# The first row maximum inside the gated unit's stage, gate inputs in token tiles, and base tiles loaded by SP's queue

## The chip, the cores and the metric

The kernel runs on one core of a Trainium2 chip. The time is device microseconds of one execution of the whole program on that core; the figure for a kernel is the median over several executions. The engines are PE (matrix multiplications), DVE (VectorE), ACT (ScalarE), POOL (GpSimd) and SP, which here only issues transfers. SP, ACT and POOL each issue DMAs, in the order of the program.

## The reference

One encoder layer over 2048 tokens of width 1024, with 16 learned meta tokens ahead of them, in float32:

```python
h = layer_norm(concat([meta, x]))
proj = h @ w_in
q, k, v, u, g_attn, g_ssm = split(proj)
q, k = apply_rope(rms_norm(q)), apply_rope(rms_norm(k))
y_attn = block_attention(q, k, v)             # 8 heads, 2 heads of keys and values, softmax over 2064 tokens
y_ssm = s5_branch(u, ...)                     # diagonal state space, then y * sigmoid(y @ w_glu + b)
merged = sigmoid(g_attn) * (y_attn @ w_attn_br) + sigmoid(g_ssm) * (y_ssm @ w_ssm_br)
h = layer_norm(ALPHA * h + merged @ w_o)
moe = sum over 16 experts of the top 256 tokens of each: (silu(t @ w_gate) * (t @ w_up)) @ w_down
out = layer_norm(ALPHA * h + moe)[16:]
```

## The kernel before

Each float32 operand of a large product is split into a high part (copied by ACT) and a low part (what DVE or POOL subtracts), and three matmuls (high by high, high by low, low by high) make one product. So ahead of each block of matmuls stand a cast on ACT and a subtraction on DVE, and ahead of these a DMA of the weights. The stages follow each other in one program; within an engine, instructions run in the order in which the code emits them, and generators (`yield`) interleave the stages by hand.

`phase_a` (0 to 300 us) norms the token tiles of 128 tokens (`ln_ops`, two `scalar_tensor_tensor` lines L106 and L107 at its end), transposes them (`trans`), and multiplies them by the columns for q, k, v (`qkv`, column group 0) and for u (`u_mm`, column group 1). `split_w(p, k)` splits the weights of column group p and row block k (L157). After the first pair of tiles a loop over `s` runs as a pipeline: transpose tile s+1, `qkv(s)`, norm of s+2, rotary positions of s-1 (`rope`), stores of s-3.

`gates` is the product for the two gates: 64 blocks of 24 matmuls of 512 columns (`pg`, L1230). It yields after every four matmuls, and the other stages call for such a quantum (`next(gg)`) wherever PE would otherwise stand, up to the first scores of attention. Its inputs are loaded back from `ht_d` in 256 KB pieces by SP.

`ssm` (317 to 752 us) is followed by `glu` (to 853.6), the gated unit, in four blocks of 512 tokens: a cast `yhi`, a subtraction `ylo` (L1133), four groups of 12 matmuls (`pz`, L1147), a sigmoid and a product `sg` per group, then a second cast and subtraction (`ylo` L1154). `glu` yields after each of these, one quantum of gate matmuls a yield.

`phase_b` is attention by units of 512 queries and one head. Ahead of the scores of a unit it needs the row maximum: 20 matmuls of queries by keys (`max_mm`, `pm`, L449), each followed by one reduction on DVE (`max_red`, L455), then four small reductions (`max_fin`) and four small matmuls with a cast (`max_put`). `pm` has two buffers, so a maximum's matmul waits for the reduction two before it. `prep_v` takes the maximum over the values (L407), transposes it on PE (L410) and scales the values. For unit 0 all of this stands between `glu` and the first scores, with gate quanta in between.

The experts run in steps of 48 matmuls (L1784, gate and up halves of one block) and down steps (L1812). The weights are 1 MB blocks `wr`, issued on SP by `load_w` (L1684) three jobs ahead and split two jobs ahead (cast L1691, subtraction L1692). From expert 9 on, side generators are advanced once per step: `finish` loads base tiles of the accumulator (`fx`, L1900), norms them and stores them to the output (L1915); `redo` fetches again the rows of an expert, norms them and stores them over the output. Results of an expert are added to `acc_d` by indirect DMAs on POOL's queue (L1834).

Of the kernel before, what the change touches and what calls it, by code (L numbers as in the profile page):

```python
# [26 lines left out]
G = 2  # L27
# [22 lines left out]
def kernel(ctx, tc, x, meta, ln_in_g, ln_in_b, w_in, q_norm_g, k_norm_g,  # L50
# [66 lines left out]
    def phase_a(start_gates):  # L117
        cr = ExitStack()
        with ExitStack() as c:
            wq = cr.enter_context(pool(name="a_q", bufs=1, side="right"))  # L120
            xp = cr.enter_context(pool(name="a_x", bufs=4, side="right"))
# [17 lines left out]
            gb = wq.tile([128, D], F32, name="gb")  # L139
            bb = wq.tile([128, D], F32, name="bb")  # L140
# [22 lines left out]
            def rope_prep(t):  # L163
                cs, sn = RC[t]
                gc, gs = (xp.tile([128, 10, 64], F32, name="gc", bufs=2), xp.tile([128, 10, 64], F32, name="gs", bufs=2))
# [126 lines left out]
            with pool(name="a_st", bufs=8) as st:  # L292
# [5 lines left out]
                for k in range(3):  # L298
                    split_w(0, k, PL)
                trans(0)  # L300
                trans(1)
                qkv(0, 0, 2)
# [20 lines left out]
            norm(2)  # L323
            for k in range(8):
                split_w(1, k, (V, PL)[k % 2])
                if k + 3 < 8:
                    load_w(wr, 1, k + 3)
                if k == 4:
                    load_rope(2)
                    load_rope(3)  # L330
# [4 lines left out]
            for s in range(NT + 4):  # L335
# [6 lines left out]
                if 1 <= s < NT:  # L342
                    trans(s + 1)
                if 0 <= s - 3 < NT:
                    qk_trans(s - 3, 0)
                next(gg, None)
                if 1 < s <= NT:
                    qkv(s, 0, 3)
                next(gg, None)
                if 0 <= s - 3 <= NT:  # L350
                    qk_trans(s - 3, 1)
                next(gg, None)
                if 2 < s + 2 <= NT:
                    norm(s + 2)
# [6 lines left out]
                if s == NT:  # L361
                    cr.close()
                    gg = start_gates()
# [8 lines left out]
    def phase_b(c):  # L372
# [6 lines left out]
        K2 = [kp.tile([128, L], F32R, name=f"k2_{g}") for g in range(G)]  # L379
        yield  # L380
# [6 lines left out]
        yield  # L387
        kp = c.enter_context(pool(name="b_v", bufs=1))
        qp = c.enter_context(pool(name="b_q", bufs=2))
        po = c.enter_context(pool(name="b_po", bufs=1, space=PSUM))  # L390
        NMT = []
        for i in range(2):
            t = kp.tile([128, 4, 128], F32R, name=f"nm{i}")
            PL.memset(f(t), 0.0)
            NMT.append(t)

        v16 = kp.tile([128, NT + 1, G, 130], F16, name="v16")
        vf = kp.tile([128, NT + 1, 128], F32, name="vf")
        mx = kp.tile([128, 1], F32, name="vmx")
# [34 lines left out]
        def load_q(n):  # L434
            qb, h = units[n]
            q1 = qp.tile([128, 512], F32R, name="q1", bufs=3)
            q2 = qp.tile([128, 512], F32R, name="q2", bufs=3)
# [1693 lines left out]
```

## Time and profile before

| | us |
|---|---|
| median of three executions | 3164.89 |
| lowest, highest | 3157.53, 3165.57 |
| the profiled execution | 3158.51 |
| its span, first to last instruction | 3156.7 |
| PE busy in it | 2978.7 (94%) |
| mean granted clock of PE | 0.977 of full |

The profiled execution is 1.81 us longer than its span, which is what lies before the first and behind the last instruction. It is 6.38 us under the median. Rows of a timeline give the start from the beginning of the span.

### The profile page before, as it was taken

To read this page: it belongs to the slowest core of one execution; us is meant where nothing else is said; L and a number is where in the kernel's file an instruction comes from. 1 tells how busy PE (TensorE), PEld (TensorE's weight loads), DVE (VectorE), ACT (ScalarE), POOL (GpSimd) and SP (SyncE) were. 2 spreads that over 40 slices of the span, in tenths; PEclk is the share of its full clock that TensorE was granted. 3 is DMA by queue.
4 is the path that set the end of the run, shared out by engine and by line. 5 is a ranking of instruction groups with operands and counts; after the bars stand their busy time and mean duration, and the time that the engine had idled before them with its cause. 6 is when DMAs were issued, how large, how long until landed. Compare 5 with 4: busy or idle time off the path is not lost.

```text
span 3156.7 us, 56179 instructions
## 1 busy us (share of the span) xinstructions
PE 2978.7 (94%) x22829; PEld 2632.0 (83%) x22829; DVE 2145.9 (68%) x3725; ACT 1572.0 (50%) x2229; POOL 1010.9 (32%) x633
## 2 busy tenths in 40 slices
PE   6999999999989999999899996799999999999997
PEld 5887787777867777777678885699999999999997
DVE  7886589783366666666466666666666665778886
ACT  2222352243369999999622222344444444666553
POOL 3221035051069999999510001111111101122221
PEclk9999999999999999999999998799999999999999
DMA  6566633557510101013366743366677667778884
GB/s 224 186 206 186 160 104 108 185 148 203 175 45 22 35 21 35 21 35 90 110 206 199 200 134 108 134 214 206 214 220 225 217 214 230 258 260 267 274 263 157
DMA packets 464499, 513.00 MB, mean 163 GB/s; under 512 B 47568, under 2 KB 387728, under 8 KB 463856
## 3 DMA queue, kind: packets, MB, share of 16 engines
q1 hardware_dynamic: 433616, 421.20, 42.7%
q0 software_dynamic: 19232, 69.53, 7.3%
q10 hardware_dynamic: 11392, 18.68, 1.7%
q8 instruction: 179, 2.93, 0.4%
q14 instruction: 80, 0.66, 0.1%
HBM read 385.59 MB, written 123.76 MB: 161 GB/s over the span
## 4 chain that ended last, share of the span: by engine, by line
PE 62%; DVE 14%; ACT 8%; DMA 6%; issue 6%; POOL 3%; SPq 1%; ACTq 0%; POOLq 0%; DVEq 0%
PE pg L1784 18%; PE pd L1812 8%; PE pg L1230 7%; PE pw L1383 5%; PE pb L1315 5%; PE pm L449 3%; PE pS L483 3%; ACT pe L490 2%; PE pS L484 2%; PE po L520 2%; DVE wl L1692 2%; PE pz L1147 1%; ACT wh L1691 1%; POOL pl L506 1%; ACT ph L502 1%
## 5 line engine op out<-in xcount | busy, mean ns | idle before, releaser
L1784 PE MATMUL pg<-xh,wh 128*128 128x256 f32 x2048 | 573.0, 280 | 5.5 <-DVE sg L1792 4.6
L1784 PE MATMUL pg<-xh,wl 128*128 128x256 f32 x2048 | 570.3, 278 | 2.8 <-DVE wl L1692 2.8
L1692 DVE TENSOR_TENSOR wl<-wr,wh 128x2048 fp32r<-128x2048 f32 x189 | 433.2, 2292 | 204.2 <-ACT wh L1691 204.1
L1784 PE MATMUL pg<-xl,wh 128*128 128x256 f32 x2048 | 570.6, 279 | 0.0
L506 POOL TENSOR_TENSOR pl<-pe,ph 128x1024 f16<-128x1024 f32 x256 | 542.5, 2148 | 60.5 <-DVE ph L500 48.8
L455 DVE TENSOR_REDUCE mx<-pm 128x1 f32<-128x412 f32 (+1 forms) x640 | 368.6, 586 | 190.1 <-PE pm L449 174.1
L1784 PEld LDWEIGHTS pg<-xh,wh 128*128 128x128 f32 x2048 | 386.6, 189 | 6.3 <-DVE sg L1792 4.8
L1784 PEld LDWEIGHTS pg<-xh,wl 128*128 128x128 f32 x2048 | 385.8, 188 | 3.5 <-DVE wl L1692 3.4
L1784 PEld LDWEIGHTS pg<-xl,wh 128*128 128x128 f32 x2048 | 386.3, 189 | 0.0
L1691 ACT CAST wh<-wr 128x2048 fp32r<-128x2048 f32 x189 | 359.8, 1904 | 16.3 <-DMA wr<-in_w_up_e_dram 9.2
L1230 PE MATMUL pg<-gh,gwh 128*128 128x512 f32 x1024 | 337.0, 405 | 19.5 <-ACT gg L1201 14.1
L490 ACT ACTIVATE pe<-pS,ebias 128x1024 f32<-128x1024 f32 x256 | 284.8, 1112 | 37.9 <-PE pS L484 37.9
L1812 PE MATMUL pd<-wh,hh 128*128 128x256 f32 x1024 | 285.8, 279 | 7.0 <-ACT ye L1831 4.6
L1812 PE MATMUL pd<-wh,hl 128*128 128x256 f32 x1024 | 283.7, 277 | 1.5 <-DVE hl L1799 1.4
L1812 PE MATMUL pd<-wl,hh 128*128 128x256 f32 x1024 | 283.1, 276 | 0.0
L1230 PEld LDWEIGHTS pg<-gh,gwh 128*128 128x128 f32 x1024 | 195.4, 194 | 62.7 <-ACT gg L1201 16.8
L502 ACT CAST ph<-pe 128x1024 f16<-128x1024 f32 x224 | 234.4, 1046 | 16.1 <-ACT pe L490 0.4
L449 PE MATMUL pm<-k,q 128*128 128x412 f32 (+1 forms) x640 | 233.5, 375 | 9.1 <-DVE mx L455 3.1
L483 PE MATMUL pS<-q,k 128*128 128x512 f32 (+1 forms) x544 | 231.8, 426 | 10.6 <-ACT pe L490 9.2
L520 PEld LDWEIGHTS <-ph 128*128 128x128 f16 (+1 forms) x2176 | 188.7, 96 | 63.6 <-issue 60.3
L520 PE MATMUL po<-v,ph 128*128 128x129 f16 (+1 forms) x2176 | 231.5, 221 | 0.8 <-ACT t L528 0.8
L522 PE MATMUL po<-v,pl 128*128 128x65 f16 (+1 forms) x2176 | 220.2, 192 | 2.2 <-POOL pl L506 2.1
(424 smaller groups left out, 6761.5 us busy)
## 6 DMA issues: line engine op xcount, KB each, us to landing
wr<-in_w_gate_e_dram SPq DMA_DIRECT2D x64, 1024.0 KB
wr<-in_w_up_e_dram SPq DMA_DIRECT2D x64, 1024.0 KB
wr<-in_w_down_e_dram SPq DMA_DIRECT2D x64, 1024.0 KB
gwr<-in_w_in_dram SPq DMA_DIRECT2D x32, 512.0 KB
gh<-ht_d SPq DMA_DIRECT2D x64, 256.0 KB
gt_d<-gg ACTq DMA_DIRECT2D x64, 256.0 KB
gt<-gt_d SPq DMA_DIRECT2D x32, 512.0 KB
q<-q_d SPq DMA_DIRECT2D x96, 128.0 KB
```

The costliest lines, as they stand in the source:

```text
L449: PE.matmul(p[:, :w], Q[n][0][:, 128 * j:128 * j + 128], K1[units[n][1] // 4][:, k0:k0 + w], start=True, stop=True)
L455: V.tensor_reduce(MX[n][:, j, c:c + 1], p[:, :w], axis=AX.X, op=OP.max)
L483: PE.matmul(p[:m, a], K2[g][:, k0:k0 + m], Q[n][1], start=True, stop=False)
L490: A.activation(e[:m, :w], p[:m, :w], AF.Exp, bias=ebias[:m], scale=HD ** -0.5)
L502: A.copy(hi[:m, :w], e[:m, :w])
L506: (PL if w == 2 else V).tensor_tensor(lo[:m, :w], e[:m, :w], hi[:m, :w], op=OP.subtract)
L520: PE.matmul(o[:, 0:129], hi[:m, a, 128 * j:128 * j + 128], v16[:m, kt, g, 0:129], start=(kt == 0 and j % 2 == 0), stop=False, skip_group_c ...
L1230: PE.matmul(p, w[:, k], h, start=(k == 0 and j == 0), stop=(k == 7 and j == 2))
L1691: A.copy(wh, wr)
L1692: V.tensor_tensor(wl, wr, f(wh), op=OP.subtract)
L1784: PE.matmul(p[:, gu], w[:, k, cs_], x[:, k], start=(k == 0 and j == 0), stop=(k == 7 and j == 2))
L1812: PE.matmul(p, a[:, k, cs_], w[:, k], start=(k == 0 and j == 0), stop=(k == 7 and j == 2))
```

## The change

Five things are changed.

1. **Start.** The first three splits of column group 0 go from POOL to DVE, in between the transpositions of tiles 0 and 1. The norm of token tile 3 is emitted in pieces among the splits of column group 1 instead of in step 1 of the loop.
2. **Gates' start.** The first two gate weights are loaded into the tiles `gb` and `bb`, and four of the first eight input pieces into token tiles (`x`), ahead of the last stores of tile 13 in SP's order; the rest of the inputs and the first two weight splits follow at the end of the same step.
3. **Row maximum of unit 0.** The pools of queries and of PSUM are opened ahead of `glu`, and `with_max` runs the 20 maximum matmuls and reductions two at a time with the last ten steps of `glu`. After `glu`, the loads of the values, the small reductions, the value maximum, and `max_put` follow, with fixed numbers of gate quanta in between. `q2` goes to two buffers and is loaded a unit later.
4. **Base tiles.** `finish` issues its loads and stores on SP's queue rather than POOL's and starts its norm two steps later.
5. **Last expert.** From step 10 of it, the side generators are advanced twice per step.

```diff
--- before.py
+++ after.py
@@ -116,7 +116,8 @@

-    def phase_a(start_gates):
+    def phase_a(cg, start_gates):
         cr = ExitStack()
+        xp = cg.enter_context(pool(name="a_x", bufs=4, side="right"))
         with ExitStack() as c:
             wq = cr.enter_context(pool(name="a_q", bufs=1, side="right"))
-            xp = cr.enter_context(pool(name="a_x", bufs=4, side="right"))
+            xg = cr.enter_context(pool(name="a_g", bufs=2, side="right"))
             px = cr.enter_context(pool(name="a_px", bufs=1, space=PSUM, side="right"))
@@ -138,4 +139,4 @@

-            gb = wq.tile([128, D], F32, name="gb")
-            bb = wq.tile([128, D], F32, name="bb")
+            gb = xp.tile([128, D], F32, name="gb", bufs=1)
+            bb = xp.tile([128, D], F32, name="bb", bufs=1)
             cols = ((0, 768), (768, 1280))
@@ -297,6 +298,7 @@
                     pass
-                for k in range(3):
-                    split_w(0, k, PL)
+                split_w(0, 0, V)
                 trans(0)
+                split_w(0, 1, V)
                 trans(1)
+                split_w(0, 2, V)
                 qkv(0, 0, 2)
@@ -323,4 +325,8 @@
             norm(2)
+            ln3 = ln_ops(sm, X[3], 128, gb, bb, "a")
             for k in range(8):
                 split_w(1, k, (V, PL)[k % 2])
+                if k > 1:
+                    next(ln3, None)
+                    next(ln3, None)
                 if k + 3 < 8:
@@ -343,12 +349,18 @@
                     trans(s + 1)
+                if s == NT:
+                    gg = start_gates(xp)
+                    next(gg)
                 if 0 <= s - 3 < NT:
                     qk_trans(s - 3, 0)
-                next(gg, None)
+                if s > NT:
+                    next(gg, None)
                 if 1 < s <= NT:
                     qkv(s, 0, 3)
-                next(gg, None)
+                if s > NT:
+                    next(gg, None)
                 if 0 <= s - 3 <= NT:
                     qk_trans(s - 3, 1)
-                next(gg, None)
-                if 2 < s + 2 <= NT:
+                if s > NT:
+                    next(gg, None)
+                if 3 < s + 2 <= NT:
                     norm(s + 2)
@@ -362,3 +374,2 @@
                     cr.close()
-                    gg = start_gates()
                     next(gg)
@@ -379,2 +390,4 @@
         K2 = [kp.tile([128, L], F32R, name=f"k2_{g}") for g in range(G)]
+        qp = c.enter_context(pool(name="b_q", bufs=2))
+        po = c.enter_context(pool(name="b_po", bufs=1, space=PSUM))
         yield
@@ -386,15 +399,3 @@
             PL.memset(f(K2[g][64:66]), 1.0)
-        yield
-        kp = c.enter_context(pool(name="b_v", bufs=1))
-        qp = c.enter_context(pool(name="b_q", bufs=2))
-        po = c.enter_context(pool(name="b_po", bufs=1, space=PSUM))
         NMT = []
-        for i in range(2):
-            t = kp.tile([128, 4, 128], F32R, name=f"nm{i}")
-            PL.memset(f(t), 0.0)
-            NMT.append(t)
-
-        v16 = kp.tile([128, NT + 1, G, 130], F16, name="v16")
-        vf = kp.tile([128, NT + 1, 128], F32, name="vf")
-        mx = kp.tile([128, 1], F32, name="vmx")

@@ -436,3 +437,2 @@
             q1 = qp.tile([128, 512], F32R, name="q1", bufs=3)
-            q2 = qp.tile([128, 512], F32R, name="q2", bufs=3)
             r, t0 = 64 * (h % 2), 512 * qb
@@ -440,6 +440,11 @@
                 SP.dma_start(f(q1[64 * i:64 * i + 64]), q_d[i, h // 2, r:r + 64, t0:t0 + 512])
-            SP.dma_start(f(q2[:64]), q_d[0, h // 2, r:r + 64, t0:t0 + 512])
-            Q[n] = q1, q2
+            Q[n] = [q1]
             MX[n] = qp.tile([128, 4, 5], F32, name="mx")

+        def load_q2(n):
+            qb, h = units[n]
+            q2 = qp.tile([128, 512], F32R, name="q2")
+            SP.dma_start(f(q2[:64]), q_d[0, h // 2, 64 * (h % 2):64 * (h % 2) + 64, 512 * qb:512 * qb + 512])
+            Q[n].append(q2)
+
         def max_mm(n, i):
@@ -557,5 +560,3 @@

-        yield 12
-        pv_ops = prep_v()
-        next(pv_ops)
+        yield
         for i in range(20):
@@ -565,8 +566,26 @@
             if i % 2:
-                yield
-            if i in (4, 9):
-                next(pv_ops)
-        red_all()
+                yield "max"
+        max_red()
+        yield "glu"
+        kp = c.enter_context(pool(name="b_v", bufs=1))
+        for i in range(2):
+            t = kp.tile([128, 4, 128], F32R, name=f"nm{i}")
+            PL.memset(f(t), 0.0)
+            NMT.append(t)
+        v16 = kp.tile([128, NT + 1, G, 130], F16, name="v16")
+        vf = kp.tile([128, NT + 1, 128], F32, name="vf")
+        mx = kp.tile([128, 1], F32, name="vmx")
+        load_v()
+        load_q2(0)
+        load_q(1)
+        yield 4
+        max_fin(0)
+        yield 4
+        pv_ops = prep_v()
+        next(pv_ops)
+        max_put(0)
+        yield 4
+        next(pv_ops)
         yield 2
-        max_put(put.pop())
+        next(pv_ops)
         for _ in pv_ops:
@@ -591,2 +610,4 @@
                 n, i = steps[s]
+                if i == 0 and n + 1 < NU:
+                    load_q2(n + 1)
                 if i == 0 and n + 2 < NU:
@@ -1161,7 +1182,28 @@

-    def gates(c):
-        hp = c.enter_context(pool(name="g_h", bufs=32, side="right"))
+    def gates(c, xp):
+        HB = {}
+        NX = 4
+
+        def load_x(b, k):
+            t = xp.tile([128, 2, 512], F32R, name="x")
+            for i in range(2):
+                SP.dma_start(f(t[:, i]), ht_d[i, k, :, 512 * b:512 * b + 512])
+            HB[b, k] = [t[:, 0], t[:, 1]]
+
+        W = {}
+
+        def load_w(i):
+            c0 = 1280 + 128 * (i % 16)
+            wr = xp.tile([128, 8, 128], F32, name="gb" if i % 2 else "bb", bufs=1)
+            SP.dma_start(wr, w_in[0, :, c0:c0 + 128].rearrange("(k p) c -> p k c", p=128))
+            W[i] = wr
+
+        load_w(0)
+        load_w(1)
+        for k in range(NX):
+            load_x(0, k)
+        yield
+        hp = c.enter_context(pool(name="g_h", bufs=32 - 2 * NX, side="right"))
         wp = c.enter_context(pool(name="g_w", bufs=2, side="right"))
         pg = c.enter_context(pool(name="g_p", bufs=2, space=PSUM, side="right"))
-        W, HB = {}, {}
         order = [(i, b) for i in range(2, 16) for b in range(2)]
@@ -1176,8 +1218,2 @@

-        def load_w(i):
-            c0 = 1280 + 128 * (i % 16)
-            wr = wp.tile([128, 8, 128], F32, name="gwr")
-            SP.dma_start(wr, w_in[0, :, c0:c0 + 128].rearrange("(k p) c -> p k c", p=128))
-            W[i] = wr
-
         def split_w(i):
@@ -1203,9 +1242,7 @@

-        load_w(0)
-        load_w(1)
-        for k in range(8):
+        for k in range(NX, 8):
             load_h(0, k)
-        yield
         split_w(0)
         split_w(1)
+        yield
         load_w(2)
@@ -1899,3 +1936,3 @@
                 xs[t] = fp.tile([128, D], F32, name="fx", bufs=4)
-                PL.dma_start(xs[t], acc_d[128 * t:128 * t + 128])
+                SP.dma_start(xs[t], acc_d[128 * t:128 * t + 128])

@@ -1904,4 +1941,4 @@
                 load(t)
-            yield
-            yield
+            for _ in range(4):
+                yield

@@ -1914,3 +1951,3 @@
                 for i in range(2):
-                    PL.dma_start(outs[t + i], xs.pop(t + i))
+                    SP.dma_start(outs[t + i], xs.pop(t + i))

@@ -1938,4 +1975,5 @@
                 sides.append(redo(e - 1, MO[2]))
-            for g in sides:
-                next(g, None)
+            for _ in range(2 if (e, s) >= (E - 1, 10) else 1):
+                for g in sides:
+                    next(g, None)

@@ -2038,2 +2076,12 @@
             drive(ssm(c))
+        def with_max(ph, ab):
+            r = None
+            for n, x in enumerate(ph):
+                if n > 14 and r != "glu":
+                    r = next(ab)
+                yield x
+            while r != "glu":
+                r = next(ab)
+                yield
+
         cb, ce, cm = ExitStack(), ExitStack(), ExitStack()
@@ -2042,3 +2090,3 @@
         with ExitStack() as c:
-            drive(glu(c, ab))
+            drive(with_max(glu(c, ab), ab))
         drive(ab)
```

Where instructions move. On DVE at the start of the program, before (`wl` is a low part of weights, `htl` of a transposed tile, `ast` to `ar` the norm's statistics):

```order
L107 SCALAR_TENSOR_TENSOR x<-x,ar,bb 128x1024 x2
L184 TENSOR_TENSOR htl<-pT,hth 128x4x128 x4
L157 TENSOR_TENSOR wl<-wr,wh 128x768 x5
L103 BN_STATS ast<-x 128x6 x2
```

and after:

```order
L107 SCALAR_TENSOR_TENSOR x<-x,ar,bb 128x1024 x2
L158 TENSOR_TENSOR wl<-wr,wh 128x768
L185 TENSOR_TENSOR htl<-pT,hth 128x4x128 x2
L158 TENSOR_TENSOR wl<-wr,wh 128x768
L185 TENSOR_TENSOR htl<-pT,hth 128x4x128 x2
L158 TENSOR_TENSOR wl<-wr,wh 128x768 x6
```

All eight splits of column group 0 now stand on DVE, the first two around the first transposed tile; POOL has none of them.

On DVE in `glu`, between two of its blocks, before (`sg` is the product behind the sigmoid, `gwl` a low part of gate weights):

```order
L1140 TENSOR_TENSOR sg<-sg,ys 128x512 x4
L1133 TENSOR_TENSOR ylo<-ys,yhi 128x2048
L1154 TENSOR_TENSOR ylo<-sg,yhi 128x2048
```

and after, in the block where the maximum begins:

```order
L1161 TENSOR_TENSOR sg<-sg,ys 128x512
L460 TENSOR_REDUCE mx<-pm 128x1
L1161 TENSOR_TENSOR sg<-sg,ys 128x512
L460 TENSOR_REDUCE mx<-pm 128x1 x2
L1161 TENSOR_TENSOR sg<-sg,ys 128x512
L460 TENSOR_REDUCE mx<-pm 128x1 x2
L1161 TENSOR_TENSOR sg<-sg,ys 128x512
L1154 TENSOR_TENSOR ylo<-ys,yhi 128x2048
L460 TENSOR_REDUCE mx<-pm 128x1 x4
L1175 TENSOR_TENSOR ylo<-sg,yhi 128x2048
L460 TENSOR_REDUCE mx<-pm 128x1 x4
```

The sixth reduction now stands behind the subtraction `ylo` of the next block, and the tenth behind that of the second product.

On SP at expert 9, where `finish` begins, before (`gb`, `bb` are the second norm's rows; in brackets the semaphores that an issue waits for, DMASW those of POOL's queue):

```order
L1894 DMA gb_22040<-in_ln_g_dram 128x1024
L1895 DMA bb_22041<-in_ln_b_dram 128x1024
L1684 DMA wr<-in_w_gate_e_dram 128x8x256 [waits DMAHW6_49,DVE_49]
L1684 DMA wr<-in_w_up_e_dram 128x8x256 [waits DMAHW7_49,DVE_49]
L1684 DMA wr<-in_w_gate_e_dram 128x8x256 [waits DMAHW0_49,DVE_49]
```

and after:

```order
L1931 DMA gb_22036<-in_ln_g_dram 128x1024
L1932 DMA bb_22037<-in_ln_b_dram 128x1024
L1721 DMA wr<-in_w_gate_e_dram 128x8x256 [waits DMAHW6_49,DVE_49]
L1937 DMA fx<-acc_d 128x1024 [waits DMASW4_49,DMASW7_49,DMASW3_49,DMASW0_49]
L1937 DMA fx<-acc_d 128x1024
L1721 DMA wr<-in_w_up_e_dram 128x8x256 [waits DMAHW7_49,DVE_49]
L1721 DMA wr<-in_w_gate_e_dram 128x8x256 [waits DMAHW0_49,DVE_49]
```

The first base tile's load stands in front of a weight load on SP, and it waits for four transfers of POOL's queue, the last scatters among them. Each later pair of stores (`out_dram<-fx`, waiting for DVE) stands between two weight loads in the same way; there are eight pairs.

## Rows read from the trace of the kernel before

**Rows 1.** The page's part 1 and two rows of part 5 (its columns stand there).

```profile
PE 2978.7 (94%) x22829; PEld 2632.0 (83%) x22829; DVE 2145.9 (68%) x3725; ACT 1572.0 (50%) x2229; POOL 1010.9 (32%) x633
...
L1692 DVE TENSOR_TENSOR wl<-wr,wh 128x2048 fp32r<-128x2048 f32 x189 | 433.2, 2292 | 204.2 <-ACT wh L1691 204.1
...
L455 DVE TENSOR_REDUCE mx<-pm 128x1 f32<-128x412 f32 (+1 forms) x640 | 368.6, 586 | 190.1 <-PE pm L449 174.1
```

**Rows 2.** Timeline of PE, the start: start, length, instruction, [idle before <- who ended it].

```profile
15.04 1.97 PE L176 MATMUL pT<-idf,x 128*128 128x128 f32 x8 [15.04 <-DVE x L107]
...
55.09 1.94 PE L176 MATMUL pT<-idf,x 128*128 128x128 f32 x8 [4.30 <-DVE x L107]
...
58.75 0.77 PE L203 MATMUL pq<-wh,hth 128*128 128x512 f32 x1 [1.73 <-DVE sq L232]
```

**Rows 3.** Timeline of DVE, the start.

```profile
12.15 5.57 DVE L107 SCALAR_TENSOR_TENSOR x<-x,ar,bb 128x1024 f32<-128x1024 f32 x2
...
24.52 1.83 DVE L157 TENSOR_TENSOR wl<-wr,wh 128x768 fp32r<-128x768 f32 x2
...
53.65 1.28 DVE L107 SCALAR_TENSOR_TENSOR x<-x,ar,bb 128x1024 f32<-128x1024 f32 x1
```

**Rows 4.** Timeline of POOL, the start.

```profile
11.37 8.03 POOL L157 TENSOR_TENSOR wl<-wr,wh 128x768 fp32r<-128x768 f32 x3 [10.92 <-ACT wh L156]
```

**Rows 5.** Windows: length; busy us (count) of PE, PEld, DVE, ACT, POOL; clock, DMA share, GB/s.

```profile
53.64:63.88 10.24, 7.07 (x23) 5.96 (x24) 9.17 (x15) 1.95 (x4) 3.63 (x2) 0.50 0.87 284
853.60:871.80 18.20, 18.17 (x80) 14.67 (x79) 4.35 (x4) 5.24 (x6) 1.19 (x3) 1.00 0.72 229
889.90:900.10 10.20, 8.14 (x20) 5.89 (x20) 7.20 (x14) 5.00 (x6) 2.40 (x2) 0.50 0.00 0
2650.00:2658.30 8.30, 8.30 (x74) 8.17 (x73) 2.43 (x2) 0.07 (x1) 2.23 (x4) 1.00 1.01 350
2661.43:2668.26 6.83, 5.26 (x24) 5.26 (x25) 5.21 (x8) 5.66 (x9) 0.00 (x0) 0.50 0.16 54
```

**Rows 6.** Timeline of PE, first gate matmuls.

```profile
325.07 1.22 PE L1230 MATMUL pg<-gh,gwh 128*128 128x512 f32 x2 [6.49 <-ACT gg L1201]
```

**Rows 7.** Timeline of ACT and its queue, same place.

```profile
317.23 2.53 ACTq L708 DMA_DIRECT2D s<-in_ssm_a_re_dram  x2
...
323.13 1.28 ACT L1201 ACT_TABLE_LOAD   x1 [5.75 <-DMA s<-in_ssm_a_re_dram]
```

**Rows 8.** Waits of PE from 853 to 897 us: us in total, times, longest.

```profile
PE pm L449 <- DMA q<-q_d: 2.9, 1, 2.9
PE pm L470 <- DVE nm L464: 1.3, 1, 1.3
PE pm L449 <- DVE mx L455: 1.1, 4, 0.5
```

**Rows 9.** Timeline of DVE, gated unit and value preparation.

```profile
815.78 2.29 DVE L1133 TENSOR_TENSOR ylo<-ys,yhi 128x2048 fp32r<-128x2048 f32 x1 [1.10 <-ACT yhi L1131]
...
873.23 2.42 DVE L407 TENSOR_REDUCE vmx<-vf 128x1 f32<-128x2176 f32 x1 [12.65 <-DMA vf<-v_d]
```

**Rows 10.** Timeline of PE, last matmul of the gated unit's third block.

```profile
812.83 0.40 PE L1147 MATMUL pz<-yhi,wl 128*128 128x512 f32 x1
```

**Rows 11.** Chain that ended last, experts: start, length, what.

```profile
2642.71 9.59 DMA acc_d<-ye,ix
...
2653.18 7.36 DMA fx<-acc_d
```

**Rows 12.** Timeline of PE, expert 9.

```profile
2663.00 0.58 PE L1784 MATMUL pg<-xh,wh 128*128 128x256 f32 x1 [4.63 <-DVE sg L1792]
```

**Rows 13.** Chain that ended last, the tail.

```profile
3137.31 1.28 DVE fa L1885
...
3140.91 3.33 DMA out_dram<-fa,io
...
3144.50 4.27 DMA out_dram<-ye,io
```

More of the change, by code (lines that the diff above doesn't have):

```diff
@@ L164, in rope_prep @@
                 cs, sn = RC[t]
-                gc, gs = (xp.tile([128, 10, 64], F32, name="gc", bufs=2), xp.tile([128, 10, 64], F32, name="gs", bufs=2))
+                gc, gs = (xg.tile([128, 10, 64], F32, name="gc"), xg.tile([128, 10, 64], F32, name="gs"))
                 PL.tensor_tensor(gc, g10, cs[:, None, :].to_broadcast([128, 10, 64]), op=OP.mult)
@@ L543, in pv_fin @@
                 PL.dma_start(y_d[512 * qb:512 * qb + 512].rearrange("(j p) d -> p j d", p=128), y)
-        load_v()
         load_q(0)
-        load_q(1)
         pend, fin, put = [], [], []
@@ L1191, in load_h @@
         def load_h(b, k):
+            if b % 2 == 0 and k < NX:
+                load_x(b, k)
+                return
             r = []
@@ L2025 @@
     cg = ExitStack()
-    gg = phase_a(lambda: gates(cg))
+    gg = phase_a(cg, lambda xp: gates(cg, xp))
     if stop <= 1:
```

## Prediction

> **What bounds the kernel.** I read the page's busy shares first: PE is busy for 2978.7 of 3156.7 us [rows 1], so the kernel is PE's, and a change can only win or lose in PE's idle stretches and in stretches where PE runs at the lower of its two clocks, 1.2 instead of 2.4 GHz (granted clock 0.50 in the windows [rows 5]). Then I went through PE's timeline for the idle time ahead of each instruction, at the five places that the change touches, and asked of each which engine ended it. At the start it is DVE's norm [rows 2, 3]. At the first gates it is ACT's evacuation, itself held up behind transfers [rows 6, 7]. Between the gated unit and attention it is a load of queries and DVE's reductions [rows 8]. In expert 9 it is the base tiles [rows 11, 12]. At the end it is two indirect stores in a row [rows 13]. The number of matmuls is the same before and after, the gate matmuls too, which are all done ahead of the first scores. So each part is costed by the PE time that it gives back or takes, against the profiled execution of 3158.51 us.
>
> **Start: about 8 us won.** PE's first transposition waits until 15.04 for the norm's last line, L107 [rows 2]. Two of these take 5.57 us, 2.8 each, while POOL runs three splits from 11.37 to 19.40 [rows 3, 4]; the same line takes 1.28 at 53.65, where POOL has no split [rows 3]. With POOL empty the first should end near 12.15 + 1.3 = 13.5, so PE starts 1.5 earlier. Most of that is lost again by 50 us, because the weights of column group 1 come in no sooner; I keep 0.5. The three splits on DVE cost 0.92 each [rows 3], 2.8 in all, beside matmuls on PE that wait only for the first of them.
>
> The larger piece is tile 3. Its transposition waits 4.30 us, to 55.09, for L107 that runs from 53.65 to 54.93 [rows 2, 3]. The norm's instructions now stand among the splits, in a stretch where DVE has idle time, and end before PE has finished `u_mm`. `rope(0)` then starts as much earlier, and `qkv(2)`, which waited another 1.73 until 58.75 for it [rows 2], comes near 53.2: 5.5 won. In the 10.24 us from 53.64 PE ran at 0.50 [rows 5] and was busy for 7.07 of them, which is 3.5 more than at the full clock. With the idle stretch gone I take 2.5 of it. Sum 0.5 + 5.5 + 2.5 = 8.5; I use 8. Low end 5.5 (the clock falls all the same), high end 9.
>
> **Gates' start: about 3 won.** The 6.49 us ahead of 325.07 [rows 6] end with an evacuation on ACT. In ACT's order five loads for `ssm` stand before it; the first issues at 317.23, and the table load behind them at 323.13, after a wait put down to such a load [rows 7]. These issues wait for earlier transfers to land. The change moves eight input pieces and two weights ahead, but adds no bandwidth, and the stores of tile 13 that these transfers are mixed with keep their place in the chain. Nothing won is the low end, the whole 6.49 the high end; I take a bit under the middle, 3, since each of the issues now waits for a transfer that started somewhat earlier.
>
> **Row maximum: about 1 won.** What it removes: PE's waits between gated unit and first scores, 2.9 + 1.3 + 1.1 = 5.3 us [rows 8], and the half clock around the first scores (8.14 us busy in the window from 889.90 at 0.50 [rows 5]; only some 4 us of it lie ahead of attention, so at most 2 are won). What it adds, in the gated unit: the last matmul of the third block ends at 813.2 [rows 10], and the subtraction `ylo` runs from 815.78 to 818.07 [rows 9]. The sixth reduction stands behind it and ends not before 818.07 + 0.59 [rows 1] = 818.7. The eighth maximum matmul needs its buffer. PE reaches it after two quanta of four gate matmuls (18.17 us for 80, 0.23 each [rows 5], so 1.8) and five maximum matmuls (about 0.2 each, an estimate from the same row at 414 columns instead of 512): 813.2 + 2.8 = 816.0. It idles for 2.7; the four reductions and the products ahead of `ylo` can push that to 3.5. I take 3. After the gated unit: the value maximum starts at 873.23, when its load has landed, and ends at 875.65 [rows 9]; I see nothing that brings the load in sooner. PE comes to the transposition that needs it after 80 gate matmuls (18.2) and four small ones (1), at 853.6 + 19.2 = 872.8, and idles 2.8. So 5.8 idle replaces 5.3, and the clock decides: 2 won ahead of attention, perhaps a bit lost behind the two new waits. I take +1, with -4 (both waits bring the low clock) and +5 (loads land early) as ends.
>
> **Base tiles: about 6 lost.** Before, `fx` stood on POOL's queue: the last scatter was issued at 2642.71 and landed 9.59 later, at 2652.3; the base tiles took 7.36 from 2653.18 [rows 11]; ACT, waiting for them in its order, held up an activation, and PE idled 4.63 us until 2663.00 [rows 12]. Starting the norm two steps later takes this wait away. But on SP the first `fx` stands ahead of a weight load and waits for the same scatters. So the weight load goes out near 2653.5 rather than in its turn. With DMA at 350 GB/s [rows 5] the 2 MB of `fx` and weights need 6.0, and 7.36 if they go as `fx` did: landed at 2659.5 to 2660.9. The cast and the subtraction behind it take at most 2.29 each [rows 1], so the low part is ready at 2664.1 to 2665.5. PE wants it in the middle of the step that began 5.4 before 2658.4, at about 2655.7: 8.4 to 9.8 idle against 4.63, so 3.8 to 5.2 lost, and I take 4, as a cast is the shorter of the two; the half clock behind it (6.83 us at 0.50 [rows 5]) stays. The second pair of loads waits for the scatters of expert 11; I put 2 on it, between 0 and 4. The stores wait for DVE's last product; the split jobs ahead give some five microseconds of cover, and I cost them at nothing.
>
> The Trainium skill speaks against this term: "DMA: Bandwidth & Descriptors", section "Issuing engines are not separate DMA queues", says that transfers issued by different engines run on the same 16 DMA engines, so that the issuing engine matters only for its own issue time. By that the move from POOL to SP is worth nothing by itself, 6 us better than my term. The trace agrees on the bandwidth, but shows the wait of POOL's `fx` for the scatter in its engine's order [rows 11], which that sentence does not cover.
>
> **The tail: 4.4 won.** The last stores go one behind the other: `fa`, issued at 3140.91, takes 3.33 to land, and then `ye` at 3144.50 [rows 13]; before them DVE does two `fa` products of 1.28 and about 1.2 among the `ye` ones. With the redo of expert 14 finished some steps sooner, `ye` follows its own norm: at most 3.6 + 2.5 = 6.1 won. Doubled side work may hold PE up by as much as 2 in steps 10 to 12. I take 4.4; ends 3 and 6.1.
>
> **Sum.** 8 + 3 + 1 - 4 - 2 + 4.4 = 10.4 won, so 3158.5 - 10.4 = 3148.1 on the profiled execution. The runs' median lies 6.4 higher and the runs spread over 8 us, so I state 3150. A difference under 0.3% of the median, 9.5 us, is not told from none.
>
> **Rivals.** *(a) This forecast*, 3143 to 3157, chance 0.50.
>
> *(b) The stalls only move*: ACT's wait at the first gates stays where the stores land (3 gone), and the gated unit's new waits bring the half clock (-4 instead of +1, so 5 gone); 10.4 - 8 = 2.4 won, about 3156 to 3160. For it: the loads are no fewer, and each wait has a successor on DVE. Against it: the start and the tail don't depend on either. Chance 0.28.
>
> *(c) SP is never held up in a way that PE feels*, the weights' cover being longer than I think: the 6 lost go, the 4.63 is won, and with it about 2.5 of the low clock behind it; 10.4 + 6 + 4.6 + 2.5 = 23.5, so 3135. This is what the skill's rule gives too. For it: 1 MB of weights needs 3 us at 350 GB/s, against 5.4 per step. Against: the scatter's 9.59. Chance 0.14.
>
> *(d) Slower: SP's order holds up the weights at each of the eight store pairs.* A store waits for DVE's last product of the norm, and the weight load behind it waits as well. It decides once each pair leaves PE idle for 3.5 us: 8 x 3.5 = 28 against 10.4 and the 9.5 of the threshold makes 3176. For it: SP issues the weights strictly in turn. Against: DVE's share is 68%, and its norm products come on time in most steps. Chance 0.08.
>
> **Range and chances.** From 3136 to 3164: it leaves out (d), half of (c) and a little of (b), 0.18 in all. Under 3155.4 (faster) lie 0.42 of (a), (c) whole and 0.04 of (b): 0.60. Within 0.3%: 0.08 of (a) and 0.24 of (b): 0.32. Slower: (d), 0.08.
>
> **What would show it.** Start: PE's transposition of tile 3 with no wait, and `qkv(2)` near 53. Gates: the 6.49 shrunk to about 3.5. Gated unit: PE waiting for a reduction once, near 816, for about 3 us, and for the value maximum near 873. Experts: in SP's order a gap of some 20 us ahead of the first `fx`, and PE idle for 8 to 9 us near 2656 waiting for a low part of weights. Tail: `ye`'s store 4 us after the last `ye` product at most. I am wrong if SP's wait shows no idle PE behind it, or if many small idle stretches appear in experts 9 to 15.

## The result, and the profile after

The changed kernel takes 3199.52 us in the median (3195.45 to 3201.1) against 3163.55 before: a ratio of 1.0115, 95% interval 1.0097 to 1.0132. It is 36 us slower, where 3150 was forecast and a range up to 3164. Its profiled execution took 3198.96, with a span of 3197.2.

Where the time went is read by the same event on PE in both traces (a start or an end in PE's timeline; the change minus before):

| event on PE | before | after | difference |
|---|---|---|---|
| first transposition | 15.04 | 13.48 | -1.6 |
| end of the last `u` matmul | 299.76 | 297.02 | -2.7 |
| first matmul of the gated unit | 779.08 | 775.59 | -3.5 |
| first scores | 894.13 | 891.30 | -2.8 |
| end of attention's last matmul | 1545.07 | 1544.94 | -0.1 |
| end of expert 8 | 2630.26 | 2630.48 | +0.2 |
| end of expert 9 | 2706.40 | 2709.20 | +2.8 |
| end of expert 11 | 2851.15 | 2863.17 | +12.0 |
| end of expert 13 | 2996.55 | 3034.12 | +37.6 |
| PE's last matmul | 3137.73 | 3186.43 | +48.7 |
| end of the span | 3156.72 | 3197.17 | +40.5 |

The first four stages win under 4 us and attention takes that back; from expert 9 on PE loses 48.5; the tail gives 8.2 back.

The waits of SP's queue in the change, from 2620 us to the end (the instruction that waited, whom for, total us, times, longest):

```profile
SPq L1937 <- DMA acc_d<-ye,ix: 49.2, 6, 13.9
SPq L1952 <- DMA out_dram<-fa,io: 43.3, 2, 25.2
...
SPq L1952 <- DVE fx L1924: 32.0, 4, 10.0
SPq L1952 <- DVE sg L1828: 28.0, 3, 9.9
...
SPq L1721 <- DMA wr<-in_w_up_e_dram: 20.3, 9, 4.0
```

L1937 is the load of a base tile, L1952 the store, L1721 a weight load. The first four rows have no counterpart before, where SP issues no base tile; the fifth had 11.9 in 4. A wait is put down to what came last. Read so, stores wait 43 us for an indirect store of rows and 84 us for DVE (eight rows in all, two are shown), loads 49 us for scatters.

One wait of a store followed through. SP's timeline, expert 12:

```profile
2852.78 0.38 SPq L1721 DMA_DIRECT2D wr<-in_w_gate_e_dram  x1
2878.47 1.15 SPq L1952 DMA_DIRECT2D out_dram<-fx  x2
2879.72 1.82 SPq L1721 DMA_DIRECT2D wr<-in_w_up_e_dram  x1
```

POOL's, DVE's, ACT's and PE's timeline at the same place:

```profile
2870.49 5.56 POOL L1927 DMA_INDIRECT out_dram<-fa,io  x1 [61.02 <-DVE oh L1760]
```

```profile
2862.74 1.28 DVE L1924 SCALAR_TENSOR_TENSOR fx<-fx,fr,bb 128x1024 f32<-128x1024 f32 x1
...
2870.51 1.28 DVE L1924 SCALAR_TENSOR_TENSOR fx<-fx,fr,bb 128x1024 f32<-128x1024 f32 x1
```

```profile
2863.58 1.91 ACT L1728 CAST wh<-wr 128x2048 fp32r<-128x2048 f32 x1
...
2889.41 1.90 ACT L1728 CAST wh<-wr 128x2048 fp32r<-128x2048 f32 x1 [18.75 <-DMA wr<-in_w_up_e_dram]
```

```profile
2891.37 0.58 PE L1821 MATMUL pg<-xh,wh 128*128 128x256 f32 x1 [10.98 <-ACT wh L1728]
...
2893.69 0.58 PE L1821 MATMUL pg<-xh,wl 128*128 128x256 f32 x1 [1.53 <-DVE wl L1729]
```

After 2852.78 SP issues nothing for 25 us: the store at 2878.47 waits for the indirect store that POOL issued at 2870.49. But the last products of the two tiles end only at 2864.0 and 2871.8, so of the wait of 25.2 us the landing alone accounts for the last 6.6; in the other wait of this kind, which ends at 3046.9, for 2.0 of 18.1. The rest would have been a wait for DVE without any landing. The weight load behind the stores goes out at 2879.72; ACT waits 18.75 us for it, and PE idles 10.98 and 1.53 us.

One wait of a load, expert 11, by the timelines of SP, ACT and PE:

```profile
2807.02 0.81 SPq L1937 DMA_DIRECT2D fx<-acc_d  x2
2808.24 0.38 SPq L1721 DMA_DIRECT2D wr<-in_w_gate_e_dram  x1
```

```profile
2818.36 1.90 ACT L1728 CAST wh<-wr 128x2048 fp32r<-128x2048 f32 x1 [12.32 <-DMA wr<-in_w_gate_e_dram]
```

```profile
2825.04 0.55 PE L1821 MATMUL pg<-xh,wh 128*128 128x256 f32 x1 [8.18 <-DVE sg L1829]
```

From 2790.4 on SP issues nothing until the scatter that these loads wait for has landed. ACT then waits for the weights behind them, and the sigmoids and products that PE waits for stand behind that cast and its subtraction: 8.18 us, put down to DVE.

The two windows around the first late weights (expert 9) and the longest idle piece (expert 12) (length; busy us of PE, PEld, DVE, ACT, POOL; clock; DMA share, GB/s):

```profile
2640.00:2662.00 22.00, 16.46 (x143) 16.17 (x141) 5.74 (x9) 5.36 (x7) 3.94 (x3) 0.91 0.77 230
2878.00:2898.00 20.00, 7.49 (x46) 7.00 (x45) 5.69 (x6) 6.77 (x9) 4.53 (x4) 0.66 1.02 313
```

In the second PE is busy for 7.49 us of 20, and the granted clock is 0.66: the lower clock comes on top of the idle time. Where [rows 12] had the wait of 4.63 us, PE now waits 5.54 for a cast of late weights, and 1.53 behind it:

```profile
2661.41 0.58 PE L1821 MATMUL pg<-xh,wh 128*128 128x256 f32 x1 [5.54 <-ACT wh L1728]
```

**Start**, answering to [rows 2, 3]. Timelines of PE, DVE, ACT and POOL:

```profile
51.32 1.07 PE L177 MATMUL pT<-idf,x 128*128 128x128 f32 x8 [0.29 <-DVE htl L185]
56.30 0.47 PE L204 MATMUL pq<-wh,hth 128*128 128x512 f32 x1 [3.91 <-DVE sq L233]
```

```profile
44.36 2.38 DVE L106 SCALAR_TENSOR_TENSOR x<-x,amv,gb 128x1024 f32<-128x1024 f32 x1
46.77 2.46 DVE L107 SCALAR_TENSOR_TENSOR x<-x,ar,bb 128x1024 f32<-128x1024 f32 x1
49.15 0.68 DVE L185 TENSOR_TENSOR htl<-pT,hth 128x512 fp32r<-128x512 f32 x1
```

```profile
49.87 0.59 ACT L184 CAST hth<-pT 128x512 fp32r<-128x512 f32 x1 [5.07 <-DVE htl L185]
```

```profile
45.61 2.54 POOL L167 TENSOR_TENSOR gc<-g,cs 128x640 f32<-128x640 f32 x1
```

Tile 3's transposition waits 0.29 rather than 4.30 us. But `qkv` now waits 3.91 for the rotary positions. L106 and L107 of the norm take 2.38 and 2.46 us, beside POOL's 2.54 for a product that took 1.56 before, and tile 2's low part (L185) stands behind them; ACT's cast waits 5.07 for that, and `rope(0)` for ACT.

**Gates**, answering to [rows 6, 7]. Timeline of PE:

```profile
309.62 0.48 PE L249 MATMUL pk<-idf,qn 128*128 128x128 f32 x1 [5.48 <-DVE ql L253]
```

```profile
321.81 0.73 PE L1267 MATMUL pg<-gh,gwh 128*128 128x512 f32 x2 [3.42 <-ACT gg L1240]
```

The wait of 6.49 is 3.42, and one of 5.48 stands ahead of it, for the low part of transposed queries; before, that wait was 1.93.

**Gated unit**, answering to [rows 8, 9]. Waits of PE from 784 to 900 us, then DVE's timeline:

```profile
PE pm L454 <- DVE mx L460: 8.0, 5, 3.4
PE pm L411 <- DVE vmx L408: 3.8, 1, 3.8
```

```profile
815.22 2.29 DVE L1154 TENSOR_TENSOR ylo<-ys,yhi 128x2048 fp32r<-128x2048 f32 x1
```

```profile
882.71 2.42 DVE L408 TENSOR_REDUCE vmx<-vf 128x1 f32<-128x2176 f32 x1 [12.63 <-DMA vf<-v_d]
...
895.51 1.72 DVE L460 TENSOR_REDUCE mx<-pm 128x1 f32<-128x414 f32 x3
```

```profile
896.15 0.46 PE L454 MATMUL pm<-k,q 128*128 128x412 f32 x1 [3.38 <-DVE mx L460]
```

PE waits for reductions 8.0 us in all: 0.5, 2.2 and 1.6 in the gated unit (one behind `ylo`, which ends at 817.5) and 3.38 in the first unit of attention, at 896.15, where DVE's value preparation stands before the reduction. For the value maximum it waits 3.8. Together 11.8, where [rows 8] had 5.3 and three shorter ones 1.4. The clock did come out better: the mean granted clock from 777 to 910 us is 0.97 against 0.95.

**Tail**, answering to [rows 13], chain of waits:

```profile
3181.03 0.50 DVE ye L1855
...
3184.80 1.30 DVE ye L1864
...
3186.36 3.31 DMA out_dram<-ye,io
```

`ye`'s store is issued 0.3 us after the last product and waits for no other landing.

### The profile page after: what moved, and what is told of

The parts are those of the page before. It is cut to its first block, busy times and chain, and to the rows that moved or that the text cites. A ratio compares the mean times of both kernels' runs of the same rounds, so it can differ in the third digit from the quotient of the medians.

```text
span 3197.2 us, 56197 instructions
## 1 busy us (share of the span) xinstructions
PE 2989.6 (94%) x22829; PEld 2643.7 (83%) x22829; DVE 2148.1 (67%) x3728; ACT 1571.4 (49%) x2229; POOL 985.7 (31%) x598
## 4 chain that ended last, share of the span: by engine, by line
PE 55%; DVE 13%; DMA 12%; ACT 10%; issue 7%; POOL 2%; SPq 1%; ACTq 0%; POOLq 0%; DVEq 0%
PE pg L1821 15%; PE pd L1849 7%; PE pw L1420 5%; PE pg L1267 5%; PE pb L1352 5%; ACT pe L495 3%; PE pm L454 3%; PE pS L488 3%; PE pS L489 2%; ACT ph L507 2%; PE po L525 2%; DVE wl L1729 1%; DMA acc_d<-ye,ix 1%; ACT wh L1728 1%; PE pz L1168 1%
## 5 line engine op out<-in xcount | busy, mean ns | idle before, releaser
L511 POOL TENSOR_TENSOR pl<-pe,ph 128x1024 f16<-128x1024 f32 x256 | 542.3, 2147 | 57.5 <-DVE ph L505 48.7
L1267 PE MATMUL pg<-gh,gwh 128*128 128x512 f32 x768 | 251.0, 403 | 8.1 <-DMA gh<-ht_d 4.3
L454 PE MATMUL pm<-k,q 128*128 128x412 f32 (+1 forms) x640 | 231.4, 372 | 11.9 <-DVE mx L460 9.7
L1871 POOL DMA_INDIRECT acc_d<-ye,ix x30 | 65.6, 2185 | 528.0 <-ACT ye L1868 516.7
```

The lines of the kernel that those rows point to most:

```text
L454: PE.matmul(p[:, :w], Q[n][0][:, 128 * j:128 * j + 128], K1[units[n][1] // 4][:, k0:k0 + w], start=True, stop=True)
L511: (PL if w == 2 else V).tensor_tensor(lo[:m, :w], e[:m, :w], hi[:m, :w], op=OP.subtract)
L1267: PE.matmul(p, w[:, k], h, start=(k == 0 and j == 0), stop=(k == 7 and j == 2))
```

## Experiments

Ratios are to the kernel before on the same chip, with 95% intervals.

**All base tiles on POOL.** The change, with

```diff
-                SP.dma_start(xs[t], acc_d[128 * t:128 * t + 128])
+                PL.dma_start(xs[t], acc_d[128 * t:128 * t + 128])
-                    SP.dma_start(outs[t + i], xs.pop(t + i))
+                    PL.dma_start(outs[t + i], xs.pop(t + i))
```

> The changed kernel with the base tiles' loads and stores issued on POOL again, everything else of the change kept (four steps ahead of the norm, doubled side steps, start, gates, row maximum). Theory A (a base tile's load or store that waits on SP holds back the weight loads behind it in SP's order): the 48.7 us that PE loses from expert 9 to its last matmul go, and with them the 4.63 us wait of before at expert 9, so about 3145 to 3160. Rival B (the side work itself, moved two steps and doubled at the end, crowds DVE and ACT): the loss stays with the queue on POOL, 3185 to 3200. Rival C (the same bytes on the same DMA engines, only the moment of transfer differs): within 10 us of the changed kernel, 3187 or more.

Measured 3161.33, ratio 0.9981 (0.9969 to 0.9994). The queue accounts for the whole loss and more; doubled steps and the later norm do not.

**The base tiles' part alone**, on the kernel before (the inverse of that edit, and four yields for two).

> The kernel before with the base tiles' part alone: loads and stores on SP, four steps ahead of the norm. Theory A: slower than before by 40 to 55 us, 3200 to 3215, as the other parts have nothing to do with the loss. Rival B: no more than 10 us slower, as the doubled side steps are missing. Also told apart: if the other parts won anything on their own, this kernel is slower than the whole change by that amount.

Measured 3200.3, ratio 1.0110 (1.0088 to 1.0132): as slow as the whole change.

**Stores on POOL, loads on SP; and the other way round.** One line each of the first edit.

> The changed kernel with the stores of the base tiles on POOL and their loads still on SP. Theory A, by SP's waits in the trace of the change (loads 49 us in 6 waits, stores about 127 us in 13, the longest 25.2 behind an indirect store of rows): most of the loss is the stores', so 3160 to 3175; the stall at 2656 for a weight (5.5 + 1.5 us) and the waits behind the scatters stay. If the loads carry the loss, 3185 or more.

> The changed kernel with the loads of the base tiles on POOL and their stores still on SP. Theory A: the stall at 2656 goes and the large one near 2880 (11 us behind the 25.2 us wait of a store) stays, 3175 to 3190. If loads carry the loss, 3150 to 3165.

Measured 3187.29, 1.0062 (1.0040 to 1.0085), and 3184.48, 1.0059 (1.0039 to 1.0079). Against all on POOL the loads cost 0.81% and the stores 0.78%. That is more together than the 1.34% that both cost, but the difference is within the intervals, so an overlap is not shown. That the stores carry most of it was wrong: each is about half.

**Later on SP.** On the change:

```diff
-            yield
+            for _ in range(4):
+                yield
             for t in range(2):
                 load(t)
...
+                for _ in range(3):
+                    yield
                 for i in range(2):
                     SP.dma_start(outs[t + i], xs.pop(t + i))
```

By the code, a base tile stored that late behind later loads can land on rows that `redo` has replaced, so that some rows of the output are older ones.

> The changed kernel, base tiles still loaded and stored by SP, but later in the code: the first loads three steps later, behind the landing of the scatter, and each pair of stores three steps after its last product. Theory A (what costs is that an SP instruction waits with weight loads behind it, not the queue that it is on): SP's waits on DVE and on the scatter at these places shrink, and 20 us or more of the 40 us go, to 3180 or less; the waits of stores for indirect stores stay in part. Rival C (transfers on SP's queue cost the weights time whatever they wait for): no change, 3195 to 3205. Rival D (the wait that matters is that of a store for an indirect store of rows): less than 15 us go.

Measured 3199.67, 1.0112 (1.0083 to 1.0141): no change. SP's waits for landings ahead of loads and stores in this kernel, from 2620 to 3140 us:

```profile
SPq L1937 <- DMA acc_d<-ye,ix: 49.8, 4, 20.0
SPq L1955 <- DMA out_dram<-fa,io: 49.5, 4, 18.9
```

The stores' waits for DVE fell from 84 to 11 us, but the loads still wait 50 for scatters, up to 20 at a time, and the stores 50 for indirect stores. The long waits have moved, not gone: SP issues nothing from 2757.7 to 2776.6 (ahead of stores), from 2846.3 to 2866.4 and from 3019.2 to 3043.9 (ahead of loads), and PE then idles 6.5 and 1.5 us at 2789, 9.8 at 2885, and 11.5 and 1.5 at 3056. The time alone fits rival C (SP's queue costs, whatever a transfer waits for); from the waits I took it that only the landings matter. The next runs show that the first is wrong and the second too narrow.

**No waits for landings.** On the change (loads from a tensor that nothing scatters to; `scr_d` is a new tensor of the output's shape, so the output lacks the base tiles):

```diff
-                SP.dma_start(xs[t], acc_d[128 * t:128 * t + 128])
+                SP.dma_start(xs[t], h1_d[128 * t:128 * t + 128])
-                    SP.dma_start(outs[t + i], xs.pop(t + i))
+                    SP.dma_start(scr_d.rearrange("(c j) d -> j c d", j=T)[t + i], xs.pop(t + i))
```

> The changed kernel, base tiles loaded and stored by SP at the same places and in the same sizes, but loaded from a tensor that nothing scatters to and stored to a scratch tensor, so that the output lacks the base tiles. No SP instruction waits for a landing of POOL's transfers any more; the stores' waits for DVE's last product stay (84 us in 13 waits in the trace of the change). Theory E (the waits for landings, 49 us on scatters and 43 on indirect stores, cost the time, those on DVE do not): the loss goes, 3155 to 3168. Theory A as first put (any wait on SP costs): about half of the loss stays, 3175 to 3185. Rival C (the bytes on SP's queue cost): 3190 or more.

Measured 3171.69, 1.0018 (1.0009 to 1.0027). **Scratch stores alone**, the loads on POOL from the accumulator:

> The changed kernel with the loads of the base tiles on POOL and their stores on SP into a scratch tensor (the output lacks the base tiles): the stores wait on SP for DVE only. Theory E: as fast as the change with all on POOL, 3155 to 3166, against 3184 with the stores on SP into the output. If waits on DVE cost, 3175 to 3185.

Measured 3174.34, 1.0027 (1.0017 to 1.0037). So without the landings about 0.97 of the 1.34% are gone, and loads on SP that wait for no scatter cost nothing (1.0018 with them there, 1.0027 without). But the second was to be as fast as all on POOL, and is 0.46% slower: the waits for DVE cost too, and the landings of indirect stores make up the other 0.32% of the stores' cost (1.0059 against 1.0027). That is 10 us, near the 6.6 and 2.0 us by which they outlast DVE's products in the trace of the change. The scratch tensors also free POOL, whose indirect stores wait 16.0 us in two waits for SP's stores in the change; these runs don't tell that share apart.

**Stores three steps later, with nothing else to wait for.** The kernel without landings, with the second half of the edit "later on SP" (three yields ahead of the stores); and the same three yields with the loads on POOL and the stores on SP into the output.

> As the kernel whose base tiles are loaded from a tensor that nothing scatters to and stored to a scratch tensor by SP (the output lacks the base tiles), with each pair of stores issued three steps behind its last product, so that SP waits neither for a landing nor, mostly, for DVE. If the stores' waits for DVE are what is left of the cost, 3155 to 3163, 8 to 12 us under that kernel. If the queue itself costs, no change, 3168 to 3176.

> As the kernel with the loads on POOL and the stores on SP into the output (0.59% slower than before), with each pair of stores issued three steps behind its last product. If the waits for DVE and for indirect stores cost apart from each other, about 12 of the 25 us that the stores cost go, to 3170 to 3176. If a store that no longer waits for DVE waits for an indirect store instead, no change, 3180 to 3188.

Measured 3148.75, 0.9947 (0.9930 to 0.9964), and 3158.52, 0.9974 (0.9963 to 0.9986). The first is lower than expected, under the kernel with all on POOL by 0.34%; it lacks the stores into the output, and with them POOL's own waits for these, which may be why; no run tests it. The second is lower than either expectation and puts SP's stores level with POOL's (0.9981): three steps take the whole 0.8% away. SP's waits in it, and, behind them, with the stores at their old place:

```profile
SPq L1954 <- DMA out_dram<-fa,io: 20.4, 3, 13.0
...
SPq L1954 <- DVE fx L1924: 9.4, 2, 7.1
```

```profile
SPq L1952 <- DMA out_dram<-fa,io: 43.4, 2, 25.3
SPq L1952 <- DVE fx L1924: 40.7, 5, 10.0
```

**The other parts alone**, each on the kernel before: two more steps ahead of the norm, on POOL; the row maximum in the gated unit; start and gates; doubled side steps.

> The kernel before with only the two further steps ahead of the base tiles' norm, all on POOL. If the wait of 4.63 us at expert 9 (with its low clock, some 2.5 more) is due to the norm coming too early for its tiles, it goes: 3 to 8 us faster than before at the last matmul of expert 9, and the same at the end unless the side work collides later, which the all-on-POOL kernel showed in experts 12 to 15 (about 10 us given back). By theory A about 0 to 5 us faster at the end.

> The kernel before with the row maximum of unit 0 in the gated unit, nothing else. My prediction had 1 us won between gated unit and first scores. The trace of the change shows waits of PE for a reduction of 0.5, 2.2 and 1.6 us in the gated unit, 3.75 for the value maximum and a new 3.4 us in the first unit behind the value preparation, 11.5 in all against 6.7 before: so 0 to 5 us slower. If the value load or the reductions are hidden in another stage, 1 to 4 us faster.

> The kernel before with the parts on the start and on the gates' first inputs, nothing else. My prediction had 8 + 3 = 11 us won. The trace of the change shows 2.7 at the end of the first stage: PE waits 3.9 us for rotary positions where 5.5 were to go. If that is all and it stays, 2 to 5 us faster; if attention, paced by several engines, gives nothing of it back and the traces of the first stages only scatter by 5 us from one execution to the next, 0 to 3.

> The kernel before with the side steps doubled from step 10 of the last expert, nothing else. My prediction had 4.4 us won. In the traces with it the time from PE's last matmul to the end is 7 to 8 us shorter, but PE's last steps are longer by 2 to 5. So 2 to 5 us faster; if the last steps pay for all of it, no change.

| part alone | median | ratio | interval |
|---|---|---|---|
| four steps ahead of the norm | 3160.37 | 0.9983 | 0.9971 to 0.9995 |
| row maximum in the gated unit | 3171.39 | 1.0015 | 1.0001 to 1.0029 |
| start and gates | 3162.11 | 0.9990 | 0.9978 to 1.0001 |
| doubled side steps | 3161.02 | 0.9985 | 0.9976 to 0.9994 |

The row maximum loses, at the edge of what is measured; start and gates cannot be told from none. With four steps ahead of the norm alone PE is 7.9 us ahead at the end of expert 9 (2698.48 against 2706.40), as the wait of [rows 12] is gone, but only 0.2 at its last matmul: later experts take it back.

**What is left of the change.** The change with base tiles on POOL and `phase_b` and `glu` as before; then the same with the stores on SP three steps late.

> What the runs so far leave of the change: parts on the start, the gates' inputs, four steps ahead of the norm and the doubled side steps, with the base tiles on POOL and the row maximum where it was. Start and gates gave 0.1%, the four steps 0.17%, the row maximum cost 0.15%, so if they add up 0.3 to 0.4% faster than before, 3152 to 3158; if the steps eat each other, about 0.2%.

> The best kernel so far (start, gates' inputs, four steps ahead of the norm, doubled side steps, row maximum where it was, base tiles loaded by POOL) with the base tiles' stores on SP, three steps behind the last product. If a store on SP that waits for nobody frees POOL's queue for scatters and gathers, 3143 to 3151, 0.5 to 0.7% under before; if it is worth nothing, 3152 to 3157, 0.3 to 0.4% under before; if the remaining waits for indirect stores (20 us in 3 waits with the stores late) cost, 3158 or more.

Measured 3153.53, 0.9961 (0.9948 to 0.9974), the fastest kernel that computes everything, and 3156.86, 0.9973 (0.9963 to 0.9983). The three parts alone give 0.17 + 0.15 + 0.10 = 0.42%, so within the intervals they add up. SP's queue is worth nothing over POOL's.

## Why the prediction was wrong

**The step that failed** is the sentence on the stores: "the split jobs ahead give some five microseconds of cover, and I cost them at nothing". The eight pairs of stores on SP cost 0.78% (about 25 us) with the loads on POOL, and 0.53% on top of the loads on SP. With the loads on POOL three steps of delay take all of it away, so it is the waiting on SP with weight loads behind it. A store waits for DVE up to 10 us, twice the cover, which is what is left of the cost with a scratch tensor (0.46%). It also waits for something that I had not looked for: the landing of an indirect store of rows into the same output, which ends the longest wait of 25.2 us and is worth 0.32%. (Both shares are uncertain by some 0.2.)

**The loads** were seen, with the right mechanism, but sized at 6 us where they cost 0.81%, about 26. At expert 9 the sum was near (5.54 + 1.53 idle; 8.4 to 9.8 forecast). I then gave the seven later pairs 2 us together; SP's loads wait six times for scatters, up to 13.9 us, and the piece of 8.18 us at 2825.04 stands behind the longest of these.

**The rival.** Rival (d), stores ahead of the weights on SP, is about half of what happened, and the loads are the other half; it had 0.08. Its 3176 was for the stores alone, 17.5 us over the profiled execution; the run with only the stores on SP took 18.4 over its own before. Not as (d) had it, though, with 3.5 us at each of eight pairs. In that run PE's idle pieces of over 0.4 us from 2600 us on add up to 34.8 us (17.3 with all on POOL), and 12.0 of that stands at one place, behind the longest wait. In the whole change they add up to 50.9, and to 17.6 before. What I held against it, DVE's share of 68%, says nothing on when one product is done. Late stores on SP take 0.9974 and stores on POOL 0.9981, so the queue itself is worth nothing; stores on SP that wait take 1.0059. The Trainium skill ("DMA: Bandwidth & Descriptors", section "Issuing engines are not separate DMA queues") says that starting DMAs on several engines saves only the sequencer's time to start them. The runs with late stores on SP and with stores on POOL agree; an issue that waits with others behind it is not in that sentence, and there the measurement decides.

**Start**: 8 forecast. The profiled traces show 2.7 at the end of the stage; with the gates 0.10% alone (interval to nothing). The transposition's wait went as forecast (0.29 left). The step that failed is "`rope(0)` then starts as much earlier": the moved norm puts 4.84 us of DVE work ahead of tile 2's low part, on which ACT's part of `rope(0)` waits. I had looked for idle time on DVE, not for what stands behind it.

**Gates**: the 6.49 shrank to 3.42 as forecast (3.5), but the wait for the queries' low part grew from 1.93 to 5.48. In this trace next to nothing is won.

**Row maximum**: +1 forecast, 0.15% (about 5 us) lost. The wait for the value maximum (2.8 forecast, 3.8) and the one behind `ylo` (3 forecast, 2.2 + 0.5) came. Two terms were missing: a second wait in the next block (1.6), and the value preparation, which now lies within attention and holds up the second unit's maximum for 3.4.

**Tail**: 4.4 forecast, 0.15% (4.8 us) measured alone. The size is right, in part by luck: in that run's trace 6.1 us are won behind PE's last matmul, the most that I allowed, but the last expert takes PE 4.6 us longer, where I had allowed 2.

**The sum**: 3148.1 for the profiled execution and 6.4 up to the median make 3154.5, so the 3150 that I stated does not follow from my own terms.

**What stays open**: why loads on SP three steps later (with the stores late) cost as much as the whole change, when late stores alone cost nothing. Its trace shows SP's waits for scatters unchanged in sum, 50 us, the longest 20, with PE idle behind them; but how much of the time is the loads' is not shown, as no run moves the loads alone. In the earlier stages single executions of the same code differ by 5.4 us at the gated unit's first matmul (775.59 in the change, 780.97 with base tiles on POOL), so the traces of start and gates settle less than their timings.

## What to carry to other kernels

Before moving a transfer to another queue, list what stands behind it there and everything that it waits for, the hazards on its DRAM tensor included; a wait longer than the prefetch cover of what follows is paid by PE, with the low clock on top. If it has to go there, issue it after its producers are done, and read the waits again: three steps were enough for the stores with the loads elsewhere, and bought nothing when the loads moved too. Moving work into an engine's idle time costs what stands behind it in that engine's order.

## What the runs showed of the hardware

On DVE the norm's two lines took 2.4 us each while POOL's products took 2.54 beside them, against 1.28 (L107, [rows 3]) and 1.56 (at 45.94 us, before) apart; even a product of 128 by 1 took 1.27 at 40.84 beside POOL's split, where the one behind it took 0.16:

```profile
40.84 1.27 DVE L93 TENSOR_TENSOR as<-ar 128x1 f32<-128x1 f32 x1
42.14 0.16 DVE L94 TENSOR_TENSOR as<-as,av 128x1 f32<-128x1 f32 x1
```

```profile
40.82 1.27 POOL L158 TENSOR_TENSOR wl<-wr,wh 128x512 fp32r<-128x512 f32 x1 [0.64 <-ACT wh L157]
```
